# A hybrid layer with a Strassen MLP: operand sums of later passes formed in the background and kept in DRAM, fourteen up-products ahead of the first down-projection, the last rows by token blocks

## The chip, the cores and the metric

The kernel runs on one core of a Trainium2 chip. The metric is the device time of one execution in microseconds; the median of several runs is compared. The core's engines are TensorE (PE, with its weight loads PEld), VectorE (DVE), ScalarE (ACT), GpSimd (POOL) and SyncE (SP), which here only issues DMAs. Each engine executes its own list of instructions in order, and waits on semaphores for what other engines or DMAs have to finish first.

## What is computed

One decoder layer on 2064 prompt tokens (16 of them meta tokens) and 8 sample tokens, width 1024, all in float32. Two mixers, an HGRN2 gated recurrence and a convolution module, are joined by `w_out`; then comes a squared-ReLU MLP of width 4096, and a last norm.

```python
def _layer(h, ...):
    hn = _rmsnorm(h, norm1_g)
    z = jnp.einsum('btd,dc->btc', hn, w_in)
    ...
    h = h + jnp.concatenate([y_hg, y_cv], axis=-1) @ w_out
    hn2 = _rmsnorm(h, norm2_g)
    h = h + jnp.square(jax.nn.relu(hn2 @ w_up)) @ w_down
    return h, s_new, new_buf
...
y_prompt = _rmsnorm(hp[:, N_META:], final_g)
y_sample = _rmsnorm(hs, final_g)
```

## The kernel before

Every product is made from two halves of each float32 number (a high part rounded for the fast matmul, and the rest), by three matmuls: high x high, high x low, low x high. So each operand exists as a pair of tiles, written by two instructions: ACT copies and rounds the high part, DVE (or POOL) subtracts it from the source for the low part. All instructions are issued through a wrapper, so that the trace shows them all at line 146; tiles tell them apart.

The first 981 us are the **mix**: input projection, recurrence, convolution, output projection. The result h goes to DRAM, transposed (`hscr`). Then the **MLP** runs in `NPASS` = 3 passes over the tokens (688, 688 and 680 columns), each through `NG` = 16 groups of 256 hidden units.

- *Up-projection.* One group is a Strassen-Winograd product: seven products U(g, 0) to U(g, 6) of 12 matmuls, 344 (or 340) columns wide, on seven sums of the weights (formed by `up_prep` for the next group, a ring of nine slots) and seven operand sums `B11, T1, T2, B22, T3, B21, T4` of the pass's tokens. The operand sums are kept for the whole pass in `op0`, `op1` and `extra` (through `bop`), in four pairs of row tiles. `h_prep(p, i)` (lines 820 to 889) loads pair i of pass p, forms its seven sums and splits each. For passes 1 and 2 it starts with the pass before it but must wait (`until ("up", p-1)`) until that pass's last up-product is done, since the operand tiles are in use until then.
- *Down-projection.* Eight units D(g, 0) to D(g, 7) for each group, 12 matmuls each, into two pairs of PSUM banks in turn (3 and 4, 5 and 6). DVE adds each unit's result onto the accumulator `acc`, which frees the bank pair. The weights are split in pass 0 (`junk` in, `wsp` out) and stored to `down_w`; passes 1 and 2 load them from there into four slots, three units ahead.
- *Order.* PE's order is written out by hand in `seq`: U and D alternate, D one group behind; the seven products of a pass's group 0 and three of its group 1 stand ahead of D(0, 0), ten in all; in group 15 the units D(14, ..) come late, so that the up-products finish early. Everything else is background work: generators kept by class `Background` with a priority (smaller goes first) and a cost model of the engines, which places the next instruction of one of them on its engine when the model finds room. `bg.until(cond)` makes it place background work until the condition holds; what it places stands in the engines' lists ahead of whatever the program emits next. The order is thus fixed when the kernel is built.
- *End of a pass.* `residual` adds h back onto `acc`; `finish` (for each tile of 128 tokens) transposes `acc` into two banks, squares and sums on ACT, forms 1/sqrt by a chain of 11 tiny DVE steps, scales and stores. The last pass splits the columns of D(15, ..) into 0 to 424 and 424 to 680, and `finish_last` does two of its tiles together.

Of the kernel before, what the change touches and what calls it, by code (L numbers as in the profile page):

```python
# [7 lines left out]
F32 = mybir.dt.float32  # L8
# [229 lines left out]
def tile_hybrid_step(  # L238
# [32 lines left out]
    ng2 = ct([P, K8], name="ng2")  # L271
    ss0 = ct([P, 5], name="ss0")
# [22 lines left out]
    xn_t = [main.tile([P, D], F32, name=f"xn{i}") for i in range(2)]  # L295
# [33 lines left out]
    def rsqrt(src, n, scale, parts=P, bufs=None, eps=None):  # L329

        x, a, y = bufs or (sc(n)[:parts], sc(n)[:parts], keep(n)[:parts])
        if eps is None:
            V.tensor_scalar(x, src, scale, EPS, ALU.mult, ALU.add)
        else:
            V.scalar_tensor_tensor(out=x, in0=src, scalar=scale, in1=eps, op0=ALU.mult, op1=ALU.add)
# [418 lines left out]
    ring, bst, bstage, acc_of = [], [], Free([], model), []  # L754
# [4 lines left out]
    def up_prep(G_):  # L759
# [4 lines left out]
        sums.update((x, bst[i // 2].rearrange("p a n -> p (a n)")[:, (i % 2) * 512:(i % 2) * 512 + 512])  # L764
                    for i, x in enumerate(("A11", "A12", "A22")))
# [30 lines left out]
    def up_first():  # L796
        steps = up_prep(0)
        late = (20, 21, 13, 14, 15, 17)
        got = yield from take(bstage, 2)
        for n_ in [n_ for n_ in range(len(steps)) if n_ not in late] + list(late):  # L800
            if n_ == late[0]:
                bstage.give(*got)
# [17 lines left out]
    def h_prep(p, i):  # L820

        n = PN[p] // 2
        yield from until(*[("h", q, d) for q in quarters(p) for d in (i, i + 4)])
        if p == 0:
            yield from region(i // 2, 4)
        else:
            yield from until(("up", p - 1))
        if p == 0 and i < 2:
            raws = yield from take(xns, 2)
        elif p == 0:  # L830
            yield from until(("mlp",))
            raws = [acc_of[0][:, 2 * i - 4 + j] for j in range(2)]
        elif i % 2:
            yield from until(("sums", p * NG), *([("bop", p, i - 2, 1)] if i > 1 else []))
            raws = raw
        else:
            raws = yield from take(xns, 2)
        yield "sp"
        for t, k in zip(raws, (i, i + 4)):
            h_load(t, p, k)  # L840
        st_ = yield from take1(bstage)
        r = {B11: raws[0][:, 0:n], B12: raws[0][:, n:2 * n], B21: raws[1][:, 0:n], B22: raws[1][:, n:2 * n]}
        s12, s1, s2, s4 = (st_[:, a, 0:n] for a in range(4))
        g, gg = g2[:, i:i + 1], g2[:, i + 4:i + 5]
        m = PROMPT[0] - NT if p == 0 else n

        def hi_(a, src, scale=1.0):
            S.activation(bop(i, 0, a)[:, 0, 0:src.shape[1]], src, AF.Copy, scale=scale)

        def lo_(a, src):  # L850
            V.tensor_tensor(bop(i, 1, a)[:, 0, 0:n], src, bop(i, 0, a)[:, 0, 0:n].bitcast(F32), ALU.subtract)

        def lo_scaled(a, src, scale):
            w = src.shape[1]
            V.scalar_tensor_tensor(out=bop(i, 1, a)[:, 0, 0:w], in0=src, scalar=scale,
                                   in1=bop(i, 0, a)[:, 0, 0:w].bitcast(F32), op0=ALU.mult, op1=ALU.subtract)

        yield "act"
        S.activation(s12[:, 0:m], r[B12][:, 0:m], AF.Copy, scale=g)
        if p == 0:  # L860
            S.activation(s12[:, m:n], hsT[:, i], AF.Copy, scale=g)
            b22s = keep(NS)
# [1132 lines left out]
```

## Time and profile before

| | |
|---|---|
| median of 3 runs | 2521.46 us (2519.86 to 2522.32) |
| the profiled execution, its own time | 2517.77 us |
| its span in the trace | 2516.1 us |
| PE busy | 2317.9 us, 92% |
| DVE / ACT / POOL busy | 1704.1 / 1056.1 / 655.1 us |
| mean DMA rate | 155 GB/s |

The page gives each engine's busy time, the span in forty slices, and groups of instructions; the trace behind it can be asked for a stretch of time by engine (what ran, for how long, and after how long a wait for whom) and for tables of busy time by stretch. The granted clock (PEclk) is TensorE's, as a share of full speed.

### The profile page before, as it was taken

Reading aid. Unit: us, or ns where it says so; the run is one execution under the profiler, and the core shown is the slowest. Engines: PE = TensorE matmul, PEld = TensorE weight load, DVE = VectorE, ACT = ScalarE, POOL = GpSimd, SP = SyncE. Lnnn points to the kernel's source line nnn. Section 1 sums busy time; section 2 is a strip of 40 time slices with the busy share of each in tenths; the row PEclk is TensorE's granted clock in tenths of the full one; section 3 lists DMA queues with packets and bytes.
Section 4 is the critical chain, followed back from the end, with each engine's and each line's share of the span. In section 5 each row is a group of like instructions: output and inputs, shape, how many; then the busy total and the mean of one; then the engine's idle time right before and its main releaser. Section 6 shows DMA issues by size and latency. Waiting matters only on the chain.

```text
span 2516.1 us, 37234 instructions
## 1 busy us (share of the span) xinstructions
PE 2317.9 (92%) x13790; PEld 2166.6 (86%) x13790; DVE 1704.1 (68%) x3129; ACT 1056.1 (42%) x2230; POOL 655.1 (26%) x511
## 2 busy tenths in 40 slices
PE   9887889989999996899999977999999889999996
PEld 8886778967877884799999976999999879999996
DVE  6797977587669444567666676666666767666655
ACT  6444644354345233544444444333333443333332
POOL 4462514443146012244333321300100013100000
PEclk9898999999999998899999997999999989999998
DMA  8764454934564466355444453434333434333332
GB/s 296 220 198 159 143 193 140 336 144 151 204 215 152 154 235 221 101 165 165 141 141 141 142 179 101 144 107 129 105 110 108 140 120 146 118 109 110 113 106 91
DMA packets 286237, 389.35 MB, mean 155 GB/s; under 512 B 19650, under 2 KB 200455, under 8 KB 269664
## 3 DMA queue, kind: packets, MB, share of 16 engines
q1 hardware_dynamic: 285912, 386.72, 47.7%
q8 instruction: 109, 1.79, 0.3%
q14 instruction: 72, 0.59, 0.1%
q10 hardware_dynamic: 144, 0.26, 0.0%
HBM read 292.14 MB, written 95.24 MB: 154 GB/s over the span
## 4 chain that ended last, share of the span: by engine, by line
PE 52%; DVE 12%; issue 6%; DMA 4%; ACT 3%; POOL 3%; SPq 1%; DVEq 0%; POOLq 0%; ACTq 0%
PE ps L146 52%; DVE ps L146 2%; DMA junk<-in_w_down_dram 2%; DVE stat L146 2%; POOL wsp L146 1%; ACT cst L146 1%; SPq L146 1%; DVE op L146 1%; DMA bst<-in_w_up_dram 1%; DVE raw L146 1%; DVE acc L146 1%; DVE xn L146 1%; DVE cst L146 1%; POOL ups L146 1%; ACT wsp L146 1%
## 5 line engine op out<-in xcount | busy, mean ns | idle before, releaser
L146 PE MATMUL ps<-op,wsp 128*128 128x512 f32 (+6 forms) x5427 | 1068.9, 352 | 33.9 <-DVE cst L146 11.4
L146 PEld LDWEIGHTS ps<-op,wsp 128*128 128x128 f32 x5427 | 897.4, 195 | 137.7 <-DVE cst L146 11.1
L146 PE MATMUL ps<-hid,wsp 128*128 128x344 f32 (+1 forms) x4536 | 769.5, 321 | 34.1 <-DVE xn L146 13.8
L146 PEld LDWEIGHTS ps<-hid,wsp 128*128 128x128 f32 x4536 | 723.4, 189 | 44.1 <-DVE xn L146 14.5
L146 DVE TENSOR_TENSOR acc<-ps,acc 128x688 f32<-128x688 f32 (+3 forms) x368 | 313.2, 851 | 278.1 <-PE ps L146 277.5
L146 ACT ACTIVATE cst<-cst 128x344 f32<-128x344 f32 (+1 forms) x384 | 188.3, 490 | 507.3 <-DVE cst L146 501.2
L146 PE MATMUL ps<-op,ups 128*128 128x344 f32 (+1 forms) x2013 | 358.3, 326 | 34.0 <-ACT op L146 15.2
L146 PEld LDWEIGHTS ps<-op,ups 128*128 128x128 f32 x2013 | 330.9, 193 | 39.5 <-ACT op L146 16.4
L146 POOL TENSOR_TENSOR scr<-scr 128x512 f32<-128x512 f32 x172 | 230.3, 1339 | 252.1 <-ACT scr L146 232.4
L146 DVE SCALAR_TENSOR_TENSOR ps<-glu,cw,ps 128x512 f32<-128x512 f32 x292 | 219.5, 752 | 6.1
L146 POOL TENSOR_TENSOR ups<-bst,ups 128x512 fp32r<-128x512 f32 x54 | 79.8, 1488 | 442.3 <-ACT ups L146 416.7
L146 DVE TENSOR_TENSOR cst<-ps,cst 128x344 f32<-128x344 f32 (+1 forms) x336 | 171.1, 509 | 30.6 <-PE ps L146 27.1
L146 POOL TENSOR_TENSOR wsp<-junk,wsp 128x256 fp32r<-128x256 f32 x128 | 104.5, 817 | 306.4 <-ACT wsp L146 279.0
L146 POOL TENSOR_TENSOR wsp<-bst,wsp 128x512 fp32r<-128x512 f32 x42 | 62.4, 1496 | 310.7 <-ACT wsp L146 287.4
L146 DVE TENSOR_TENSOR hid<-cst,hid 128x344 fp32r<-128x344 f32 (+1 forms) x192 | 104.6, 545 | 52.6 <-ACT hid L146 51.6
L146 DVE TENSOR_TENSOR ups<-raw,ups 128x512 fp32r<-128x512 f32 x108 | 79.7, 738 | 73.1 <-ACT ups L146 72.9
L146 ACT ACTIVATE scr<-glu,cw 128x512 f32<-128x512 f32 x188 | 125.2, 715 | 1.9 <-DVE glu L146 1.9
L146 POOL TENSOR_TENSOR wsp<-raw,wsp 128x1024 fp32r<-128x1024 f32 (+1 forms) x34 | 78.7, 2314 | 79.6 <-ACT wsp L146 68.1
L146 DVE TENSOR_TENSOR wsp<-raw,wsp 128x512 fp32r<-128x512 f32 x84 | 61.7, 735 | 53.1 <-ACT wsp L146 53.0
L146 ACT ACTIVATE hid<-cst 128x344 fp32r<-128x344 f32 (+1 forms) x192 | 94.2, 491 | 6.1
L146 ACT ACTIVATE wsp<-raw 128x512 fp32r<-128x512 f32 (+1 forms) x118 | 85.9, 728 | 16.9 <-DMA raw<-in_w_in_dram 9.7
L146 ACT ACTIVATE wsp<-junk 128x256 fp32r<-128x256 f32 x128 | 52.0, 408 | 92.2 <-DMA junk<-in_w_down_dram 73.3
(231 smaller groups left out, 2133.3 us busy)
## 6 DMA issues: line engine op xcount, KB each, us to landing
wsp<-kw SPq DMA_DIRECT2D x96, 1024.0 KB, 4.8
wsp<-down_w SPq DMA_DIRECT2D x250, 256.0 KB, 2.7
bst<-in_w_up_dram SPq DMA_DIRECT2D x144, 256.0 KB, 4.2
kw<-wsp SPq DMA_DIRECT2D x32, 1024.0 KB, 5.7
down_w<-wsp SPq DMA_DIRECT2D x128, 256.0 KB, 2.4
junk<-in_w_down_dram SPq DMA_DIRECT2D x128, 128.0 KB, 2.3
raw<-in_w_in_dram SPq DMA_DIRECT2D x24, 512.0 KB, 7.2
raw<-in_w_up_dram SPq DMA_DIRECT2D x48, 256.0 KB, 3.2
```

The source lines that it names most:

```text
L146: return fn(*args, **kw)
```

## The change

- The accumulator `acc` moves to the main pool; in the mix its memory serves as the scratch buffers, of which there are then ten instead of eleven. The two `xn` tiles become wider, and the separate tile for the mask row goes.
- Pass 0: sums and most splits of its operands are emitted product by product (`h_first`, `h_rest`).
- Passes 1 and 2: `h_stage(p)`, added at U(2, 0) of the pass before with the last priority, loads the h rows, forms the 28 pairs of operand tiles (four pairs of rows by seven sums) one after another in one tile `stg`, and stores each to DRAM (`bop_d`). At each U(15, k) of passes 0 and 1 the background is first run until the staging is complete, and then `h_fetch` loads the operands of product k, whose tiles the old pass has just used for the last time, by four DMAs.
- `seq`: group 1's seven products all precede D(0, 0), so that fourteen products stand ahead of it; group 15 alternates like the others in passes 0 and 1. In the last pass group 15's products come in a row, then D(14, ..) and D(15, ..) together on columns 0 to 424, then both on 424 to 680.
- `finish` takes two neighbouring banks and works on 1024 columns at once (one square, one scaling), and the 1/sqrt is a power on POOL, in `finish_last` too. `residual` starts when all eight tiles of `acc` have been written once.

```diff
+    def split_sum(hi, lo, src, scale):
+
+        yield "act"
+        S.activation(hi, src, AF.Copy, scale=1.0 if scale is None else scale)
+        yield "dve"
+        if scale is None:
+            V.tensor_tensor(lo, src, hi.bitcast(F32), ALU.subtract)
         else:
-            raws = yield from take(xns, 2)
+            V.scalar_tensor_tensor(out=lo, in0=src, scalar=scale, in1=hi.bitcast(F32),
+                                   op0=ALU.mult, op1=ALU.subtract)
...
+        def h_stage(p):
+
+            n = PN[p] // 2
+            x, xx = yield from take(xns, 2)
+            t1, t2 = x[:, 2 * NT:2 * NT + n], xx[:, 2 * NT:2 * NT + n]
+
+            def emit(i, idx, src, scale):
+                yield from split_sum(stg[:, 0, 0:n], stg[:, 1, 0:n], src, scale)
+                yield "sp"
+                SP.dma_start(bop_d[p - 1, i, idx], flat32(stg))
+
+            for i in range(4):
+                yield "sp"
+                h_load(x, p, i)
+                h_load(xx, p, i + 4)
...
+                yield from emit(i, B11, b11, g)
+                yield from emit(i, B21, b21, gg)
+                yield from emit(i, B22, b22, gg)
+                V.tensor_tensor(t1, b12, b11, ALU.subtract)
+                S.activation(t2, b22, AF.Copy, scale=gg)
+                yield from emit(i, T1, t1, g)
...
+            xns.give(x, xx)
+            done.add(("staged", p))
+
+        def h_fetch(p, idx):
...
+            for i in range(4):
+                src = bop_d[p - 1, i, idx].rearrange("p (a n) -> p a n", a=2)[:, :, 0:n]
...
+                    o = (i % 2) * 12 + idx
+                    SP.dma_start(ops_t[i // 2].rearrange("p (s n) -> p s n", n=NT)[:, o:o + 7:6, 0:n].bitcast(F32), src)
+                done.add(("bop", p, i, idx))
...
         def finish(p, i, c0_, n):
...
-            for j in range(2):
-                S.activation(junk16[:n, 0:512], ps[0:n, bs[j], :], AF.Square, accum_out=s2[:, j:j + 1])
+            ss, r_ = sc(1)[:n], keep(1)[:n]
+            S.activation(junk16[:n], row, AF.Square, accum_out=ss)
+            yield "dve"
+            V.scalar_tensor_tensor(out=ss, in0=ss, scalar=1.0 / D, in1=emm[:n, p, i:i + 1], op0=ALU.mult, op1=ALU.add)
+            yield "pool"
+            G.tensor_tensor(r_, ss, mhalf[:n, 0:1], ALU.pow)
...
                 if g == 1:
-                    seq += us[0:3] + [x for i in range(4) for x in (ds[i], us[3 + i])] + ds[4:]
-                elif g == NG - 1:
-                    seq += [us[0], ds[0], us[1], us[2], ds[1], us[3], us[4], ds[2], us[5], us[6]] + ds[3:]
+                    seq += us + ds
+                elif g == NG - 1 and p == NPASS - 1:
+                    seq += us
...
-            seq += [D_(NG - 1, d, bl) for bl in bls for d in range(K8)]
+            seq += [D_(g, d, bl) for bl in bls for g in range(NG - 1 if p < NPASS - 1 else NG - 2, NG) for d in range(K8)]
...
                 run_unit(product(p, g, d), lambda p=p, g=g, d=d: up_epilogue(p, g, d))
+                if g == 2 and d == 0 and p < NPASS - 1:
+                    bg.add(h_stage(p + 1), 7)
+                if g == NG - 1 and p < NPASS - 1:
+                    bg.until(lambda: ("staged", p + 1) in done)
+                    h_fetch(p + 1, PRODUCTS[d][3])
```

How this moves instructions is seen at three places. The first is DVE at the end of pass 0: the acc additions `acc<-ps,acc` there belong to D(13, 6), D(13, 7) and D(14, 0), `hid`, `cst` and `ups` to the up-projection. Before:

```order
L146 TENSOR_TENSOR acc<-ps,acc 128x688
L146 TENSOR_TENSOR hid_7714<-cst,hid_7714 128x344
L146 TENSOR_TENSOR acc<-ps,acc 128x688 x2
L146 TENSOR_TENSOR cst<-ps,cst 128x344 x2
L146 TENSOR_TENSOR raw_85<-bst_7386,raw_84 128x512
L146 TENSOR_TENSOR raw_84<-raw_84,bst_7387 128x512
L146 TENSOR_TENSOR acc<-ps,acc 128x688
```

And after, from D(13, 6)'s addition on; the rows up to the next addition of `acc` go on in the same manner, with six more splits into `stg`:

```order
L146 TENSOR_TENSOR acc<-ps,acc 128x688
L146 TENSOR_TENSOR hid_7724<-cst,hid_7724 128x344
L146 TENSOR_TENSOR acc<-ps,acc 128x688
L146 SCALAR_TENSOR_TENSOR stg<-xn_90,vec,stg 128x344
L146 SCALAR_TENSOR_TENSOR xn_91<-xn_90,ng_78,xn_91 128x344
L146 TENSOR_TENSOR stg<-xn_91,stg 128x344
L146 SCALAR_TENSOR_TENSOR xn_90<-xn_91,vec 128x344
L146 TENSOR_TENSOR stg<-xn_90,stg 128x344
L146 SCALAR_TENSOR_TENSOR xn_91<-xn_90,ng_78,xn_91 128x344
L146 TENSOR_TENSOR stg<-xn_91,stg 128x344
L146 SCALAR_TENSOR_TENSOR stg<-xn_90,vec,stg 128x344
```

Between D(13, 7)'s addition and D(14, 0)'s, which were neighbours, now stand eleven splits into `stg` with the sums that they need.

The second place is SP's list of DMAs in the same part of the program. Before, storing the split down weights (`down_w<-wsp`), loading the next (`junk<-in_w_down_dram`) and loading h rows for the operand sums alternate:

```order
L146 DMA junk<-in_w_down_dram 128x2x128
L146 DMA down_w<-wsp_86 128x512
L146 DMA junk<-in_w_down_dram 128x2x128
L146 DMA raw_84<-hscr 128x688
L146 DMA raw_85<-hscr 128x688
L146 DMA down_w<-wsp_86 128x512
L146 DMA junk<-in_w_down_dram 128x2x128
L146 DMA down_w<-wsp_86 128x512
L146 DMA junk<-in_w_down_dram 128x2x128
```

After, from the last store of the staging on:

```order
L146 DMA bop_d<-stg 128x688 x7
L146 DMA op_83<-bop_d 128x2x344 x2
L146 DMA op_84<-bop_d 128x2x344 x2
L146 DMA raw_85<-in_w_up_dram 128x4x128
L146 DMA bst_7385<-in_w_up_dram 128x4x128 x2
L146 DMA bst_7386<-in_w_up_dram 128x4x128
L146 DMA down_w<-wsp_87 128x512
L146 DMA junk<-in_w_down_dram 128x2x128
L146 DMA op_83<-bop_d 128x2x344 x2
L146 DMA op_84<-bop_d 128x2x344 x2
L146 DMA down_w<-wsp_87 128x512
L146 DMA junk<-in_w_down_dram 128x2x128
```

The loads of the h rows and the sums are gone from here; each product's four fetches (`op<-bop_d`) stand ahead of the next pair of weight DMAs, and so on for all seven products.

The third place is PE at the start of pass 1: `ident,acc` are the transposes of `finish`, `hid,wsp` the first down-units, `op,wsp` and `op,ups` the up-products. Before, the end of the tenth product, the last transposes and D(0, 0), with the next product behind it:

```order
L146 MATMUL ps<-op_82,wsp_87 128x344 x6
L146 MATMUL ps<-op_83,wsp_87 128x344 x6
L146 MATMUL ps<-op_82,wsp_88 128x344 x6
L146 MATMUL ps<-op_83,wsp_88 128x344 x6
L146 MATMUL ps<-ident,acc 128x128 x8
L146 MATMUL ps<-ident,acc 48x128 x8
L146 MATMUL ps<-hid_7713,wsp_86 128x344 x6
L146 MATMUL ps<-hid_7714,wsp_86 128x344 x6
L146 MATMUL ps<-op_82,wsp_88 128x344 x6
L146 MATMUL ps<-op_83,wsp_88 128x344 x6
```

After, the end of the fourteenth product, the last transposes and the first down-units:

```order
L146 MATMUL ps<-op_83,wsp_88 128x344
L146 MATMUL ps<-op_84,wsp_88 128x344
L146 MATMUL ps<-op_83,wsp_88 128x344
L146 MATMUL ps<-extra,wsp_88 128x344 x9
L146 MATMUL ps<-ident,acc 48x128 x8
L146 MATMUL ps<-hid_7723,wsp_87 128x344 x6
L146 MATMUL ps<-hid_7724,wsp_87 128x344 x6
L146 MATMUL ps<-hid_7723,wsp_87 128x344 x6
L146 MATMUL ps<-hid_7724,wsp_87 128x344 x6
```

Four more products stand ahead of the first down-unit, and the down-units of group 0 follow each other.

## Rows read from the trace of the kernel before

**Rows 1.** The page, part 1: busy time, share, instructions; then part 2's row.

```profile
PE 2317.9 (92%) x13790; PEld 2166.6 (86%) x13790; DVE 1704.1 (68%) x3129; ACT 1056.1 (42%) x2230; POOL 655.1 (26%) x511
...
PE   9887889989999996899999977999999889999996
```

**Rows 2.** Table of stretches, PE to POOL busy with instruction counts, clock, DMA.

```profile
core 0: us, PE busy (x) PEld busy (x) DVE busy (x) ACT busy (x) POOL busy (x), PEclk, DMA share, GB/s
0.00:981.00 981.00, 902.24 (x5004) 774.25 (x5004) 698.85 (x1375) 438.00 (x927) 368.16 (x263) 0.95 0.59 199
981.00:1041.00 60.00, 29.59 (x123) 24.93 (x124) 40.28 (x82) 30.06 (x72) 7.21 (x8) 0.66 0.34 95
...
1445.40:1494.00 48.60, 45.17 (x273) 42.52 (x272) 35.58 (x55) 21.10 (x48) 15.56 (x18) 1.00 0.57 179
1494.00:1554.00 60.00, 31.82 (x170) 27.93 (x168) 45.68 (x141) 27.18 (x64) 2.93 (x2) 0.76 0.37 123
1554.00:1955.00 401.00, 397.45 (x2493) 396.63 (x2494) 253.31 (x392) 147.94 (x287) 52.09 (x36) 0.99 0.39 116
...
1998.00:2050.60 52.60, 31.22 (x169) 28.26 (x167) 42.98 (x138) 24.83 (x60) 3.01 (x2) 0.75 0.36 111
...
2491.00:2516.10 25.10, 6.03 (x29) 3.87 (x28) 15.77 (x73) 7.36 (x22) 0.00 (x0) 0.58 0.29 111
```

**Rows 3.** Time line of PE around the first change of pass.

```profile
1458.59 2.05 PE L146 MATMUL ps<-hid,wsp 128*128 128x344 f32 x12
1460.47 2.07 PE L146 MATMUL ps<-op,wsp 128*128 128x344 f32 x12
...
1464.27 7.72 PE L146 MATMUL ps<-hid,wsp 128*128 128x344 f32 x48
...
1494.01 1.11 PE L146 MATMUL ps<-op,wsp 128*128 128x344 f32 x6
...
1511.19 0.94 PE L146 MATMUL ps<-op,wsp 128*128 128x344 f32 x2 [4.78 <-DVE op L146]
...
1554.04 3.81 PE L146 MATMUL ps<-hid,wsp 128*128 128x344 f32 x12 [6.79 <-DVE xn L146]
```

**Rows 4.** The page, part 5: groups of instructions, mean ns after the comma.

```profile
L146 DVE TENSOR_TENSOR acc<-ps,acc 128x688 f32<-128x688 f32 (+3 forms) x368 | 313.2, 851 | 278.1 <-PE ps L146 277.5
...
L146 DVE TENSOR_TENSOR hid<-cst,hid 128x344 fp32r<-128x344 f32 (+1 forms) x192 | 104.6, 545 | 52.6 <-ACT hid L146 51.6
...
L146 ACT ACTIVATE hid<-cst 128x344 fp32r<-128x344 f32 (+1 forms) x192 | 94.2, 491 | 6.1
```

**Rows 5.** The page, part 6: DMA issues, KB each and us to landing.

```profile
kw<-wsp SPq DMA_DIRECT2D x32, 1024.0 KB, 5.7
down_w<-wsp SPq DMA_DIRECT2D x128, 256.0 KB, 2.4
```

**Rows 6.** DMA issues from 1470 to 1560 us, columns as in rows 5.

```profile
raw<-hscr SPq DMA_DIRECT2D x4, 344.0 KB, 5.2
```

**Rows 7.** Table of a busy stretch in the mix, columns as in rows 2.

```profile
440.00:480.00 40.00, 39.12 (x328) 38.54 (x328) 28.97 (x59) 17.93 (x38) 19.31 (x11) 1.00 0.99 318
```

**Rows 8.** Time line of the end, PE and DVE.

```profile
2484.13 1.25 PE L146 MATMUL ps<-ident,acc 128*128 128x128 f32 x10
...
2499.86 1.97 PE L146 MATMUL ps<-ident,acc 128*128 128x128 f32 x8 [5.31 <-DVE xn L146]
...
2502.83 0.16 DVE L146 SCALAR_TENSOR_TENSOR stat<-stat,emm 128x1 f32<-128x1 f32 x1
...
2505.20 1.41 DVE L146 SCALAR_TENSOR_TENSOR xn<-ps,kept,fg 128x512 f32<-128x512 f32 x2
...
2511.18 1.40 DVE L146 SCALAR_TENSOR_TENSOR xn<-ps,kept,fg 40x512 f32<-40x512 f32 x2
```

**Rows 9.** Time line of the hand-over to the MLP: SP's queue and PE.

```profile
1002.23 12.06 SPq L146 DMA_DIRECT2D emm<-mscr  x19
...
1026.44 3.81 PE L146 MATMUL ps<-op,wsp 128*128 128x344 f32 x12 [6.52 <-DVE cst L146]
```

More of the change, by code (lines that the diff above doesn't have):

```diff
@@ L914, in tile_hybrid_step, with h_rest @@
+    def h_rest():
+        yield from until(("sum0", 2), ("sum0", 3))
+        yield from region(1, 4)
+        for idx in SUMS[:-1]:
+            yield from first_split((2, 3), idx)
+        yield from until(("mlp",))
+        yield from first_split(range(4), T4)
+        xns.give(*xn_t[:2])
+        bstage.give(*bst)
+        done.add(("rest",))
     with tc.manual_schedule():
@@ L916, in tile_hybrid_step @@
         G.memset(ones, 1.0)
+        G.memset(mhalf, -0.5)
         with ExitStack() as p1:
@@ L1587, in tile_hybrid_step @@
         hid = [[mlp_p.tile([P, 2, 2 * NT], F32R, name=f"hid{a}{b}") for b in range(2)] for a in range(2)]
-        msb = mlp_p.tile([P, 2 * NT], F32, name="msb")
-        acc = mlp_p.tile([P, K8, 2 * NT], F32, name="acc")
-        acc_of.append(acc)
+        stg = mlp_p.tile([P, 2, NT], F32R, name="stg")
+        up_raws[1] = [b[:, 0:512] for b in scr.take(3)]
         done[("mlp",)] = model.t["pe"]
@@ L1628, in residual @@
         def residual(p):
-            yield from until(*[("st", q) for q in quarters(p)])
+            yield from until(*[("st", q) for q in quarters(p)], *[("acc", p, k) for k in range(K8)])
+            t, msb = yield from take(xns, 2)
             yield "sp"
@@ L1637, in residual @@
             for k in range(K8):
-                yield from until(("acc", p, k))
-                t = yield from take1(xns)
                 yield "sp"
@@ L1677, in finish @@
             xns.give(t)
         def finish_last(p, i, c0_):
-            bs = yield from bank(4)
+            pair = []
+            while not pair:
+                pair = [b for b in (0, 2) if b in banks.items and b + 1 in banks.items] if 4 in banks.items and \
+                    7 in banks.items else []
+                if not pair:
+                    yield "poll"
+            bs = [4, pair[0], 7, pair[0] + 1]
+            for b in bs:
+                banks.items.remove(b)
             ts = raw
@@ L1725, in finish_last @@
             bg.add(last_gains(), 9)
-            r_ = yield from rsqrt(ss, 2, 1.0 / D, eps=emm[:, p, i:i + 2])
+            r_ = keep(2)
+            V.scalar_tensor_tensor(out=ss, in0=ss, scalar=1.0 / D, in1=emm[:, p, i:i + 2], op0=ALU.mult, op1=ALU.add)
+            yield "pool"
+            G.tensor_tensor(r_, ss, mhalf, ALU.pow)
+            yield "dve"
             yield from until(("gains", 2))
```

258 lines of the change are left out of this document (124 added, 134 removed).

## The prediction

> **What bounds the kernel now.** I read the page first: TensorE (PE) is busy 2317.9 us of 2516.1, and its row in forty slices is full except for a few places [rows 1]. The table of stretches sizes those places [rows 2]. Steady MLP work has next to no slack: 397.45 busy us in the 401.00 from 1554 to 1955. At the two changes of pass PE is busy 31.82 of 60.00 us and 31.22 of 52.60, at a mean granted clock of 0.76 and 0.75 of full speed. The last 25.10 us hold 6.03 us of PE, and where the mix hands over (981 to 1041) it has 29.59 of 60.00. So a gain has to come from one of those holes, and anything that stops PE in steady work is paid in full. The time line of PE gives the unit: 12 matmuls 344 wide, an up-product or a down-unit, start 1.88 us apart (1458.59 to 1460.47), while the same 12 take 3.81 us when they follow a wait [rows 3].
>
> **Where the background work went.** Before, the operand sums of the next pass are formed at the pass change, and PE waits on DVE and ACT for them (the 4.78 us ahead of 1511.19). After, they are formed during the running pass through one tile, `stg`, and stored. The order on DVE decides how much of that is hidden: of the 28 splits of pass 1's operands, 17 stand among pass 0's work and 11 stand together between the acc addition of D(13,7) and that of D(14,0), since the planner is made to finish them after U(15,0). In pass 1 it is 23 and 5. DVE runs its list in order, so D(14,0)'s bank stays full until all 11 are through. PE can still issue U(15,0), D(14,0), U(15,1), D(14,1), U(15,2): 5 x 1.88 = 9.4 us. Then D(14,2) needs that bank.
>
> **What one split costs.** ACT writes the high part, DVE the low, the tile is stored, and the next split may write only when the store has landed. The same operations on 344 columns take 0.491 us (ACT) and 0.545 us (DVE) [rows 4]. A store of two 128 x 344 tiles is 344 KB; a store of 256 KB lands in 2.4 us and one of 1024 KB in 5.7 [rows 5], so between them 2.4 + 88/768 x 3.3 = 2.8. With 0.15 us for the hand-overs a cycle is 0.49 + 0.55 + 2.8 + 0.15 = 4.0 us. Eleven cycles are 44; the last store need not have landed (-2.8); the next pair's two rows must come in between, 5.2 us at a pass change [rows 6], part of it under the last splits of the old pair, so +3; the first acc addition of 0.851 us [rows 4] closes it: about 45 us after D(13,7). PE has work for 9.4, so it stops for **36.5 us** (31 with cycles of 3.5, 48 with 5). In pass 1, five cycles, no new pair: 20 - 2.8 + 0.85 + 2.2 for the rest of the store that the first of them waits for = 20.2, less 9.4: **10.8 us** (8 to 16).
>
> **What the fetches cost.** After each U(15,k) come four DMAs, 4 x 344 KB = 1.41 MB, on SP, and SP's order puts them ahead of the next down-projection weight. Pass 0 then still stores one weight piece and loads one (256 KB and 128 KB, 0.39 MB) for every unit, and the group's up-weights, 1.05 MB, go through the same queue. From the end of the staging to the last fetch that is 7 x 1.80 + 1.05 = 13.7 MB. A busy stretch of the mix moves 318 GB/s at a DMA share of 0.99 [rows 7], so 320 is what I take: 43 us. The weight for D(15,2) comes after the seventh fetch, and the units that PE can do before it, from D(14,2) on, are twelve: 23 us. PE waits the difference, **20 us**; in pass 1 there is no w_down load or split, 7 x 1.66 + 1.05 = 12.6 MB, 40 us against 23: **17 us**. Both between 10 (if the four weight slots stand fuller than SP's order says) and 24 (280 GB/s). The Trainium skill (DMA: Bandwidth & Descriptors, section Bandwidth) has 425 GB/s for one 16 MB transfer into SBUF; by that figure, an estimate, the queue would last 32 us and the waits be 9 and 7, but the row shows 318 with the engines full.
>
> **What the pass change gives back.** From 1494.01 to the first down-unit of pass 1 at 1554.04 PE passes 60.0 us [rows 3] and does ten products (10 x 1.88 = 18.8) and 48 transposes (4.8 us at 0.1 each, from ten in 1.25 with the last one's drain [rows 8]): 36.4 us are lost. After, 14 products need no sums, and only the finishing of pass 0's rows (transposes, ACT square, DVE scale) stands beside them, with 26.4 us of products to hide it. I leave 7.5 us of waits: six finishing tiles, of which four can be under the products, and one unit at half clock. Gain **29 us**; bounds 22 and 34. The 52.6 us of the second change [rows 2] hold the same work, 29.0 lost: gain **21 us** (15 to 27). The thirteen down-units before the first change take 29.7 us (1464.27 to 1494.01) where 13 x 1.88 is 24.5 [rows 3], since DVE forms sums among their additions: **5 us** more.
>
> **What the end gives back.** From 2491.00 to 2516.10 the last tiles finish one after another: transposes at 2499.86, scale at 2505.20, the last tile's scale at 2511.18, some 6 us for each tile [rows 8], 2.4 of it (2502.8 to 2505.2) a chain of tiny DVE steps that a power on POOL replaces. After, tiles 0 to 3 belong to columns 0 to 424, whose D(15) units are done while 16 units on 256 columns still run, so they finish under PE work; only tiles 4 and 5 stay behind the last unit. That leaves a last addition, transposes, squares, the power, the scale and a store: 8.5 us by the durations of the same steps. Against it, PE has 2.6 us of transposes inside its work and 1.5 us for the narrower units. 25.1 - 8.5 - 2.6 - 1.5 = **12.5 us** (9 to 14). POOL's power on one or two columns stands in no row; the smallest and dearest bounds are a DVE step of 0.16 us and some 2 us, the chain it replaces: I take 0.7, inside the 8.5.
>
> **The rest.** The 40 splits that lie in steady work add 0.5 us each on ACT and DVE, which have room (253.31 and 147.94 us busy in 401.00) [rows 2]; each can still hold ACT or DVE for the landing of the previous store when two stand close, and PE can run two units ahead: **+4 us** (0 to 12). Two more restarts of PE after a wait, 3.81 - 1.88 = 1.9 us each [rows 3]: **+4**. The mix has ten scratch buffers where it had eleven, and three conv taps move from ACT to DVE: 0, but 8 us either way, since PE's 902.24 us there leave 79 us of waits that a new order may move [rows 2]. The hand-over to the MLP still waits for 19 small loads of `emm` that occupy SP 12.06 us and hold the up-weights back (PE's 6.52 us ahead of 1026.44) [rows 9]; the first sums are ready earlier but that queue is not: 0 (-6 to +3). The two pairs that come before the first down-unit are counted in the pass change.
>
> **Sum**, against the profiled execution's own 2517.77 us: +36.5 + 10.8 + 20 + 17 = 84.3 of new waits; -29 - 21 - 5 - 12.5 = -67.5; +4 + 4. Net +24.8: 2542.6. That execution lies 3.7 us under the median of the runs, 2521.46, so on the runs' scale **2546 us**, 1.0% slower. A difference under 0.2%, 5 us, is one that a measurement of this kernel can't tell from none.
>
> **Rivals.** *The fetches hold nothing back.* If weights come through between them (four slots ahead, DMA at a share of only 0.57 there [rows 2]), the 37 us go and 2509 us, faster, is left. Against it: SP's order, and seven times 1.41 MB in a stretch that has 0.39 MB a unit now. The Trainium skill (same page, section Queues, rings and completion order) says that descriptors of one ring are consumed in ring order, which no row here shows and which would speak against this rival. *The lump is short too*: if a store lets go of the tile in well under 1 us, or the staging is through by U(15,0), all 84 us go: 2462, or 2480 if half of the price of the fetches stays, the change doing what it says. Against it: 2.4 us for smaller stores [rows 5]. *The pass change still waits.* The row sums of pass 0 can't be finished before its last addition, and D(0,0) may not write `acc` before the last transposes; if residual additions and squares pile up on DVE and ACT at that place as now, 40 of the 50 us stay lost: 2586 us, slower. It decides from the point where finishing six tiles takes DVE and ACT more than the 26.4 us of products.
>
> **How the numbers follow.** My sum 0.63 (with its bounds 2522 to 2572), fetches free 0.18, all short 0.07, pass change as before 0.12. Range: the low end takes in the free fetches with some luck in the mix, 2503; the high end the third rival, 2586. Faster: the rivals with free fetches and a sliver of the sum, 0.23; within 5 us of now 0.08; slower 0.69.
>
> **What would show it.** After U(15,2) of pass 0 PE stands still some 36 us, with the releaser DVE acc, while ACT and DVE show eleven `stg` pairs 4 us apart; after it, waits on weights (ACT or POOL wsp in pass 0, DMA wsp in pass 1) of 20 and 17 us, with DMA shares over 0.9. Fourteen products then run with under 10 us of gaps. The last addition of acc lies 8 to 9 us before the end. I am wrong if `stg` pairs lie under 2 us apart, if the DMA share in the fetch stretch stays near 0.6 with no PE wait, or if the pass change keeps 30 us of gaps.

## The result, and the profile after

The changed kernel takes **2561.68 us** (median of 4 runs, 2560.96 to 2564.89) against 2521.63 us for the kernel before (4 runs, 2519.86 to 2522.32): a ratio of 1.0162, 95% interval 1.0145 to 1.018. It is 1.6% slower; the forecast was 2546 us, 1.0% slower. Its profiled execution took 2564.89 us, 47.1 us more than that of before; the medians are 40.0 us apart, so 7 us of the difference between the two traces is scatter from one execution to the next.

To see where, both traces are cut at the same work. Every group's last up-product U(g, 6) ends in nine matmuls on the tile `extra`, and what is done between two such places is the same in both kernels if they are chosen well: U(2, 6) to U(14, 6) is the inside of a pass, U(14, 6) to U(2, 6) of the next pass a pass change with both its sides. The times between them, read from the starts of those matmuls, with the sum that the prediction's terms make for the same stretch:

```
                           before    after   change   forecast
start to U(2,6), pass 0    1087.2   1089.5    +2.3      0
inside of pass 0            352.3    363.6   +11.3     +4, all three passes
change from pass 0 to 1     163.3    187.3   +24.0     36.5 + 20 + 2 - 29 - 5 = +24.5
inside of pass 1            345.6    349.9    +4.3
change from pass 1 to 2     150.4    162.8   +12.4     10.8 + 17 + 2 - 21     =  +8.8
inside of pass 2            341.4    342.7    +1.3
U(14,6) of pass 2 to end     75.9     67.5    -8.4     -12.5
span                       2516.1   2563.2   +47.1     +24.8
```

The page of the changed kernel, part 1, and part 6's row of the new stores, answers to [rows 1] and [rows 5]:

```profile
PE 2326.5 (91%) x13790; PEld 2170.7 (85%) x13790; DVE 1684.5 (66%) x2906; ACT 1055.4 (41%) x2199; POOL 666.1 (26%) x529
...
bop_d<-stg SPq DMA_DIRECT2D x56, 344.0 KB, 2.7
```

PE's busy time is nearly the same (8.6 us more); some 38 us of waiting have come in, though DVE has less to do. The store lands in a median of 2.7 us, where 2.8 had been worked out from [rows 5]. Where PE waits is seen on its time line at the end of pass 0 (after [rows 3]):

```profile
1467.74 2.07 PE L146 MATMUL ps<-op,ups 128*128 128x344 f32 x12
1501.11 3.78 PE L146 MATMUL ps<-hid,wsp 128*128 128x344 f32 x12 [31.30 <-DVE acc L146]
...
1513.51 3.81 PE L146 MATMUL ps<-op,ups 128*128 128x344 f32 x12 [4.42 <-DVE cst L146]
...
1528.90 2.34 PE L146 MATMUL ps<-hid,wsp 128*128 128x344 f32 x12 [1.17 <-ACT wsp L146]
1535.83 5.82 PE L146 MATMUL ps<-hid,wsp 128*128 128x344 f32 x24 [4.59 <-DVE acc L146]
1542.86 12.45 PE L146 MATMUL ps<-hid,wsp 128*128 128x344 f32 x72 [1.21 <-ACT wsp L146]
1555.14 3.46 PE L146 MATMUL ps<-op,wsp 128*128 128x344 f32 x21
```

The line at 1467.74 is U(15, 2), the fifth unit that could be issued; D(14, 2) starts 31.30 us after it had ended, released by the addition of D(14, 0). In that time ACT does this (its time line):

```profile
1478.28 0.58 ACT L146 ACTIVATE stg<-xn,vec 128x344 fp32r<-128x344 f32 x1 [5.18 <-DMA xn<-hscr]
1481.81 0.58 ACT L146 ACTIVATE stg<-xn,vec 128x344 fp32r<-128x344 f32 x1 [2.96 <-DMA bop_d<-stg]
1485.33 0.58 ACT L146 ACTIVATE stg<-xn,vec 128x344 fp32r<-128x344 f32 x1 [2.94 <-DMA bop_d<-stg]
```

One split each 3.5 us, most of it the wait for the store before it. In pass 1, where five are left, the same place reads:

```profile
2016.25 3.81 PE L146 MATMUL ps<-hid,wsp 128*128 128x344 f32 x12 [10.62 <-DVE acc L146]
2019.86 2.60 PE L146 MATMUL ps<-op,wsp 128*128 128x344 f32 x12
2027.34 3.78 PE L146 MATMUL ps<-hid,wsp 128*128 128x344 f32 x12 [4.88 <-DVE raw L146]
```

The table of stretches (columns as in [rows 2]) shows what follows: the stretch of the fetches, the new pass's fourteen products, and the fetches of pass 1.

```profile
1501.00:1555.10 54.10, 42.60 (x216) 40.42 (x217) 23.58 (x34) 14.55 (x31) 13.63 (x16) 0.83 0.93 310
1555.10:1598.90 43.80, 34.80 (x218) 32.72 (x217) 25.75 (x44) 21.89 (x43) 6.09 (x7) 0.95 0.33 109
...
2016.20:2069.30 53.10, 42.12 (x217) 40.95 (x218) 24.03 (x34) 9.77 (x19) 2.97 (x2) 0.83 0.87 292
```

The first is 18 units, 33.8 us of matmuls at 1.88 us each, in 54.0 us (D(14, 2) at 1501.11 to the next pass's first product at 1555.14), with the DMA engines 93% busy at 310 GB/s. Of the 20.2 us more, PE is idle for 11.4, in the four waits shown above behind the one of 31.30; the rest is units that run at a granted clock of 0.50 behind a wait, as the one at 1501.11, 3.6 us long. In pass 1 the same 18 units take 53.0 us, and three of the waits are for down weights:

```profile
2044.83 3.65 PE L146 MATMUL ps<-hid,wsp 128*128 128x344 f32 x12 [2.22 <-DMA wsp<-down_w]
...
2050.22 2.12 PE L146 MATMUL ps<-hid,wsp 128*128 128x344 f32 x12 [1.74 <-DMA wsp<-down_w]
2054.42 15.02 PE L146 MATMUL ps<-hid,wsp 128*128 128x344 f32 x84 [2.08 <-DMA wsp<-down_w]
2069.28 3.89 PE L146 MATMUL ps<-op,ups 128*128 128x340 f32 x24
```

The second row of the table answers to the 60.0 us of [rows 2], with four more products in it: 43.8.

### The profile page after: what moved, and what is told of

It reads as the page before. It is cut to its first block, busy times and chain, and to the rows that moved or that the text cites. A ratio compares the mean times of both kernels' runs of the same rounds, so it can differ in the third digit from the quotient of the medians.

```text
span 2563.2 us, 37257 instructions
## 1 busy us (share of the span) xinstructions
PE 2326.5 (91%) x13790; PEld 2170.7 (85%) x13790; DVE 1684.5 (66%) x2906; ACT 1055.4 (41%) x2199; POOL 666.1 (26%) x529
## 4 chain that ended last, share of the span: by engine, by line
PE 46%; DVE 20%; issue 11%; DMA 10%; ACT 5%; POOL 4%; SPq 2%; POOLq 0%; ACTq 0%; DVEq 0%
PE ps L146 46%; DVE ps L146 7%; DMA junk<-in_w_down_dram 4%; SPq L146 2%; DVE stat L146 2%; POOL wsp L146 2%; DMA bst<-in_w_up_dram 2%; DVE acc L146 2%; ACT cst L146 1%; DMA bop_d<-stg 1%; DVE cst L146 1%; POOL ups L146 1%; DVE I L146 1%; DVE kept L146 1%; DVE raw L146 1%
## 5 line engine op out<-in xcount | busy, mean ns | idle before, releaser
L146 PE MATMUL ps<-hid,wsp 128*128 128x344 f32 (+2 forms) x4512 | 779.9, 324 | 95.3 <-DVE acc L146 61.9
L146 DVE TENSOR_TENSOR acc<-ps,acc 128x688 f32<-128x688 f32 (+4 forms) x424 | 346.5, 818 | 319.4 <-PE ps L146 259.6
L146 POOL TENSOR_TENSOR acc<-acc 128x512 f32<-128x512 f32 x169 | 225.1, 1332 | 244.4 <-ACT acc L146 227.6
L146 DVE TENSOR_TENSOR cst<-ps,cst 128x344 f32<-128x344 f32 (+1 forms) x336 | 170.9, 509 | 19.2 <-PE ps L146 15.7
L146 ACT ACTIVATE acc<-glu,cw 128x512 f32<-128x512 f32 x185 | 123.5, 715 | 1.6 <-DVE glu L146 1.6
L146 ACT ACTIVATE wsp<-raw 128x512 fp32r<-128x512 f32 (+1 forms) x118 | 85.9, 728 | 10.8 <-DMA raw<-in_w_in_dram 6.6
```

Of the source, the lines that this page charges most:

```text
L146: return fn(*args, **kw)
```

## The experiments

Two theories stood behind the forecast: the splits left over at U(15, 0) run at the pace of the store's landing and hold PE (the lump); and the fetches hold the weights of the following down-units. Twelve kernels were run. All are edits of the changed kernel, but for two that start from the kernel before. The stretches of the table above are used throughout; the spans are those of one profiled execution each, and a time given without an interval is that of a single execution. Such stretches scatter by some 3 us: the inside of pass 2, which no edit concerns, took 340.3 to 343.5 us in all fourteen kernels.

**No operands formed at all.** The staging and the fetches leave; the rest of the change stays.

```diff
-                    bg.add(h_stage(p + 1), 7)
...
-                    bg.until(lambda: ("staged", p + 1) in done)
-                    h_fetch(p + 1, PRODUCTS[d][3])
+                    for i in range(4):
+                        done.add(("bop", p + 1, i, PRODUCTS[d][3]))
```

> The changed kernel without the staging and the fetches: passes 1 and 2 take pass 0's operand sums as they stand in the tiles, so the forming, storing and fetching of their own is left out. Theory (the two lumps of staging and the fetches ahead of the weights hold PE): the waits of 33 + 11 us and 20 + 19 us at the ends of passes 0 and 1 go, and some 8 us inside the passes: 2562 - 91 = 2471 us, PE without a wait over 2 us from U(15,0) to the end of either pass. Rival (the down weights or the up weights hold PE there anyway, as group 15 now runs alternating): waits of 10 us or more stay in those stretches and the time is over 2500.

2461.59 us, with the kernel before at 2523.99: the theory's side, 9 us below its figure, and the longest wait of PE left there is 2.1 us. The pass changes took 135.6 and 129.7 us (187.3 and 162.8 in the changed kernel), the insides of passes 0 and 1 356.7 and 343.2 (363.6 and 349.9). So without any work on the operands of passes 1 and 2, which the kernel before still does, the change would be 62 us faster than it, and staging and fetching cost 100 us of run time; of the 103 us by which the spans differ, 85 lie at the two pass changes, 14 inside passes 0 and 1.

**Two staging tiles.** The splits alternate between `stg` and the unused end of `bst1`; the order stays.

```diff
+                stg = stgs[sn[0] % 2]
+                sn[0] += 1
                 yield from split_sum(stg[:, 0, 0:n], stg[:, 1, 0:n], src, scale)
```

> The changed kernel with two staging tiles in turn; the order on all engines stays, eleven and five splits still stand together. Theory (each split waits for the landing of the store before it, 3.5 us a cycle): a cycle falls to 1.75 us, PE's wait for D(14,0)'s addition from 31 to 12 to 15 us in pass 0 and from 10.6 to about 4 in pass 1, the fetch waits stay at 20 and 19: 2562 - 23 = 2539 us. Rival (the splits' own instructions and their hand-overs take the 3.5 us): cycles stay over 3 us and the time at 2555 to 2562.

2541.41 us. PE's time line at the same two places of this kernel:

```profile
1485.55 3.45 PE L146 MATMUL ps<-hid,wsp 128*128 128x344 f32 x12 [16.62 <-DVE acc L146]
...
1993.85 3.60 PE L146 MATMUL ps<-hid,wsp 128*128 128x344 f32 x12 [3.37 <-DVE acc L146]
```

16.6 and 3.4 us where it was 31.3 and 10.6. All engines' lists are the same in both kernels, and the lump lost 15 and 7 us with the second tile: the landing of the stores set its pace. What is left is the splits' own chain and one wait of 5.5 us for the next pair's rows.

**Even staging.** One tile; over the 49 up-products of groups 8 to 14 the number of splits that must have been placed rises evenly to 28.

```diff
+                if 8 <= g < NG - 1 and p < NPASS - 1:
+                    quota = -(-28 * ((g - 8) * 7 + d + 1) // (7 * (NG - 1 - 8)))
+                    bg.until(lambda: nst[p + 1] >= quota)
```

> The changed kernel with one staging tile, but the planner is made to place one or two splits beside each up-product of groups 8 to 14, so that none is left at U(15,0). Theory (the cost is that eleven and five stand in front of one acc addition): the waits of 31 and 10.6 us go, the even splits cost 0 to 6 us a pass inside, the fetch waits stay at 20 and 19: 2562 - 36 = 2526 us. Rival (each split stops ACT and DVE for the landing of the store before it wherever it stands, and PE with them): the same 40 us return as many waits of 0.5 to 2 us in groups 8 to 14, 2555 us or more.

2559.17 us: the theory missed, and the rival's time came (its reason, the landing, did not bear out, as the kernels with all three mends show below). The pass changes fell from 187.3 and 162.8 to 153.5 and 148.8, but the insides rose from 363.6 and 349.9 to 393.1 and 362.7. The 31 us that were seen in one piece came back in small ones. What PE waited for from 1240 to 1462 us, groups 8 to 14 of pass 0, in the kernel with even staging (engine, line, for whom; us, times, longest); in the changed kernel the waits in these groups come to 7.2 us:

```profile
PE ps L146 <- ACT wsp L146: 12.7, 5, 3.7
PE ps L146 <- DVE acc L146: 6.8, 4, 4.0
PE ps L146 <- DVE cst L146: 2.8, 1, 2.8
```

**Late fetches.** One fetch DMA goes behind each following unit.

```diff
         def h_fetch(p, idx):
+            fpend.extend((p, idx, i) for i in range(4))
...
+            h_fetch_next()
             for f in old:
                 f()
```

> The changed kernel with the fetches issued one DMA behind each following unit instead of four at once behind each up-product; the lumps stay. Theory (seven times four fetches stand ahead of the weights on SP): the waits on weights of 20 and 19 us fall under 5 us each, the lumps of 31 and 10.6 stay: 2562 - 32 = 2530 us. Rival (the DMA engines are full in that stretch, whatever the order): the waits stay, or move to the first products of the next pass, 2550 us or more.

2542.10 us, between the two. The change from pass 1 to 2 fell from 162.8 to 145.5 us; the one from pass 0 to 1 only from 187.3 to 183.7. Not all of the 17.3 us is the fetches': the planner left four splits instead of five behind D(13, 7)'s addition, and PE's wait for D(14, 0)'s was 4.26 us instead of 10.62. The 18 units from D(14, 2) to the next pass took 48.2 and 43.6 us (54.0 and 53.0 in the changed kernel).

**No fetches, staging kept.**

```diff
-                    h_fetch(p + 1, PRODUCTS[d][3])
+                    for i in range(4):
+                        done.add(("bop", p + 1, i, PRODUCTS[d][3]))
```

> The changed kernel with the staging and its stores but without the fetches: passes 1 and 2 take pass 0's operand sums from the tiles. Theory (the fetches hold the weights and so PE at the ends of passes 0 and 1): the two lumps stay (PE's waits of 31 and 10.6 us), behind them the waits on weights go, and from U(14,6) to U(2,6) of the next pass 187 us become 170 and 163 become 142: 2562 - 38 = 2524 us. Rival (what the late-fetch run gained, 20 us, is all that the fetches cost): 2540 us.

2539.45 us, the rival's time. The change from pass 1 to 2 took 142.0 us, 20.8 less than in the changed kernel; the one from pass 0 to 1 only 3.2 less. Neither is the price of the fetches, since the planner placed other work differently too. In pass 1 four splits are left instead of five, and the lump is shorter. In pass 0 the waits between U(14, 6) and U(0, 6) fell by 14.4 us (71.2 + 53.9 against 66.4 + 44.3), but the next stretch, to U(2, 6), rose by 11.3, where this kernel's last transposes stand later in PE's order and wait for the scaling of the tile before. PE in pass 0 and pass 1:

```profile
1503.13 3.78 PE L146 MATMUL ps<-hid,wsp 128*128 128x344 f32 x12 [31.52 <-DVE acc L146]
...
1548.91 3.94 PE L146 MATMUL ps<-op,wsp 128*128 128x344 f32 x24
...
1586.38 1.09 PE L146 MATMUL ps<-ident,acc 128*128 128x128 f32 x8 [3.06 <-DVE xn L146]
1590.14 3.68 PE L146 MATMUL ps<-ident,acc 128*128 128x128 f32 x16 [2.66 <-DVE xn L146]
1596.51 1.06 PE L146 MATMUL ps<-ident,acc 128*48 128x128 f32 x8 [2.69 <-DVE xn L146]
...
2006.79 3.81 PE L146 MATMUL ps<-hid,wsp 128*128 128x344 f32 x12 [6.73 <-DVE acc L146]
...
2048.22 5.78 PE L146 MATMUL ps<-op,ups 128*128 128x340 f32 x36
```

The price is read from the 18 units between, D(14, 2) to the next pass's first product, which stand in the same order in all these kernels. With the kernel without operands and the one with room, two tiles and fetches at once (below) all four cases of lump and fetches are there:

```
18 units, start to start, us                pass 0                     pass 1
lump and fetches (changed kernel)           1501.11-1555.14  54.0      2016.25-2069.28  53.0
lump, no fetches (this kernel)              1503.13-1548.91  45.8      2006.79-2048.22  41.4
fetches, no lump (room, two tiles)          1485.26-1532.53  47.3      1988.78-2031.25  42.5
neither (no operands formed)                1456.84-1494.81  38.0      1933.98-1968.74  34.8
```

So the fetches cost 8.2 and 11.6 us behind a lump, 9.3 and 7.7 without one: 17 to 20 us in both passes together. And the lump leaves another 7 to 11 us behind its own wait, with fetches or without. Each case is one execution, so 3 us here or there mean little.

**All three mends, and the same with one tile.** Even staging and late fetches, with two tiles and with one.

> The changed kernel with all three: two staging tiles, splits placed evenly in groups 8 to 14, fetches one DMA behind each unit. Theory (what even staging cost with one tile, 28 us in pass 0 and 15 in pass 1, was ACT standing at the next split for the landing of the store before it, with the down weights' splits behind it): with two tiles that store is an older one and has landed, groups 8 to 14 lose at most 6 us a pass more than without staging, the lumps are gone and the fetch waits as in the late-fetch run: 2490 to 2510 us, faster than before. Rival (the splits' own work on ACT and DVE is too much there): the 43 us stay, about 2537 us.

> The same with one staging tile. Theory of the landing: the 28 + 15 us of the even-staging run stay, 2559 - 22 = 2537 us, 30 us or more above the run with two tiles. Rival (work, not landing): the same time as with two tiles within 8 us.

2530.32 us (ratio to before 1.0039, 1.0026 to 1.0051) with two tiles, 2529.0 us with one: spans 2527.1 and 2527.3. The theory missed: the engines' lists are the same in both, and with splits spread evenly the second tile is worth nothing; the inside of pass 0 stays at 391.1 and 392.5 us. The pass changes are short, 149.7 and 133.0 us with two tiles. In the one with two tiles, ACT's waits in the same stretch hold none for the landing of a store; the first after those for DVE's `cst` are

```profile
ACT wsp L146 <- DMA junk<-in_w_down_dram: 21.6, 11, 3.9
ACT bst L146 <- DMA xn<-hscr: 11.0, 2, 10.3
ACT stg L146 <- issue: 8.1, 2, 5.2
```

A forced split is written into ACT's and DVE's lists at once, in front of other work, and waits there for its own sources, once 10.3 us for the rows of the next pair. How such a wait reaches PE is seen in three lines of this kernel, DVE, ACT and PE in turn:

```profile
1406.85 1.03 DVE L146 TENSOR_TENSOR bst<-xn,bst 128x344 fp32r<-128x344 f32 x1 [2.02 <-ACT bst L146]
```

```profile
1409.37 1.01 ACT L146 ACTIVATE cst<-cst 128x344 f32<-128x344 f32 x2 [2.55 <-DVE cst L146]
```

```profile
1411.26 3.81 PE L146 MATMUL ps<-hid,wsp 128*128 128x344 f32 x12 [3.41 <-ACT wsp L146]
```

DVE stands 2.02 us for the split's high part from ACT, with additions to `cst` behind it; ACT stands 2.55 us for one of these, with a weight split (`wsp`) behind it; and PE waits 3.41 us for that and then runs its next unit at a granted clock of 0.50, 3.81 us long. That chains like this one make up the whole of the 34 us by which the inside of pass 0 exceeds the run without operands was not shown.

**Placed where the planner finds room, one tile.** The planner is told not to count the landing; nothing is forced, and all 28 splits are placed by group 11.

```diff
+                t_ = model.cur.t
                 SP.dma_start(bop_d[p - 1, i, idx], flat32(stg))
+                model.cur.t = t_
```

> The changed kernel with one line: the planner no longer counts the landing of a store before the next split, so that all 28 splits are placed where it finds room, by group 11, and none is left at U(15,0) in either pass; one tile, fetches as in the changed kernel. Theory (forcing puts a split in front of waiting ACT and DVE work, room does not): groups 2 to 14 lose at most 10 us a pass more than without staging, the ends of the passes lose the lumps, 43 to 8 and 21 to 4 us: 2562 - 52 + 10 = 2520 us. Rival (a split costs PE 0.5 to 1 us wherever it stands, as in the even-staging runs): 28 + 15 us are lost inside and the time is 2550 us or more.

2577.59 us, the slowest of all: the pass changes are at 146.2 and 138.1, the insides at 418.7 and 374.5.

**The same with two tiles, fetches at once and late.**

> The run with room, two tiles and late fetches, but with four fetches at once behind each up-product as in the changed kernel; no lump stands before them. Theory (order on SP): the waits on weights come back in full, 15 to 20 us in each pass, 2509 + 35 = 2544 us. Rival (the number of bytes, not their order, sets that wait): 2509 to 2515 us.

> The same with two staging tiles and the fetches one DMA behind each unit. Theory: inside the passes under 10 us in both together over the run without operands, and the ends of the passes as in the run of the three mends (150 and 133 us from U(14,6) to U(2,6), against 136 and 130 without operands): 2462 + 10 + 18 = 2490 us, the fastest so far. Rival (a split costs 0.5 to 1 us wherever it stands): 2520 us.

2524.32 us with fetches at once, 2509.27 us with late ones (ratio to before 0.9939, 0.9921 to 0.9957). The first differs from the kernel with one tile in the second tile alone, with the same lists on all engines, and is 53 us faster: inside pass 0 381.8 us against 418.7. What ACT waited for from 1200 to 1470 us, first with one tile, then with two:

```profile
ACT stg L146 <- DMA bop_d<-stg: 82.4, 19, 9.0
```

```profile
ACT bst L146 <- DMA bop_d<-bst: 12.3, 3, 5.2
ACT stg L146 <- DMA bop_d<-stg: 9.1, 3, 3.9
```

So the landing counts wherever splits follow each other closely in the lists, in a lump or in the open, and not where they are spread: in the run with even staging, one tile and late fetches the last 21 stores of pass 0 go out from 1302 to 1481 us, one in nine microseconds. Late fetches against fetches at once: 142.5 and 132.4 us at the pass changes against 146.2 and 137.9, and 15 us in the run time, less than half of what the theory of order asked for and more than the rival's 6; only 9 of the 15 lie at the pass changes, the rest where the fetches have no part. Without operands these stretches took 135.6 and 129.7. So fetches at once, with no lump before them, cost 11 and 8 us at the pass changes, and late ones 7 and 3.

**Fourteen products alone, in the kernel before.**

```diff
                 if g == 1:
-                    seq += us[0:3] + [x for i in range(4) for x in (ds[i], us[3 + i])] + ds[4:]
+                    seq += us + ds
```

> The kernel before with nothing changed but seven instead of three products of group 1 ahead of D(0,0), fourteen in all. Theory (at a pass change PE waits first for the operand sums, 34 and 24 us, then for the last rows of the old pass, 15 and 13 us; the order helps the second alone): 16 to 24 us of the two second waits go, the first stay: 2524 - 20 = 2504 us. Rival (the four more products only wait for their own sums, and both waits are one): 2518 us or more.

2525.58 us against 2520.75 of the kernel before: no gain. The pass changes took 165.9 and 151.5 us (163.3 and 150.4 before). The products are issued ahead of D(0, 0), but the old finish is not done by then; PE at that place in this kernel:

```profile
1563.51 1.05 PE L146 MATMUL ps<-ident,acc 128*48 128x128 f32 x4 [4.66 <-DVE xn L146]
1571.52 17.64 PE L146 MATMUL ps<-hid,wsp 128*128 128x344 f32 x96 [6.96 <-DVE xn L146]
```

**Fourteen products, the new finish and the new end, in the kernel before.** The change's `finish`, `finish_last` and order of the last pass are put in as well; the operand sums stay as they were.

> The kernel before with fourteen products ahead of D(0,0), the changed finish (neighbouring banks, one square, the power on POOL) and the changed order of the last pass, without any staging or fetch. Theory (these parts bring gains by themselves, and the staging is what costs): 2504 - 8.5 for the end (29.0 us lost behind the last product before, 20.5 after) = 2495 us, and a few us less at the pass changes by the shorter finish. Rival (the gains need the operands to be ready): 2512 us or more.

2502.34 us, ratio to before 0.9926 (0.9911 to 0.9941), between the theory's 2495 and the rival's 2512. The pass changes take 156.9 and 145.9 us and the end 67.7 instead of 75.9. D(0, 0) no longer waits for a scaling; the one wait over 1 us left among the group's eight down-units is

```profile
1564.17 11.60 PE L146 MATMUL ps<-hid,wsp 128*128 128x344 f32 x72 [1.09 <-ACT acc L146]
```

This version and the one with room, two tiles and late fetches beat both kernels. They were not measured side by side, and their intervals overlap, so which of them is faster stays open.

## Why the prediction was right, and where its sizes were off

**The lump: right.** The forecast was 36.5 us in pass 0 and 10.8 in pass 1; PE waited 31.30 and 10.62 behind the named bank, with the named releaser. (The terms given for pass 0 add up to 35.7, not 36.5.) The cycle was 3.5 us where 4.0 had been taken: 0.58 on ACT and a wait of 2.94, of which DVE's 0.58 is part, so 2.4 us are left for store and hand-overs where 2.95 had been taken. The run with two tiles shows the cause. What the forecast did not have is that the lump also leaves 7 to 11 us behind it, in units at the lower clock and in waits; it had one restart of 2 us in each pass.

**The fetches: half the price, and the sum met by luck.** 20 and 17 us had been forecast, and the two stretches did lose 20.2 and 19.2 us (54.0 and 53.0 for 33.8 of work). But without the fetches the same units still take 45.8 and 41.4 us. The fetches' own share is 8.2 and 11.6, in pass 0 below the stated bound of 10; the rest is what the lump leaves behind, 7.8 and 6.7, and 4.1 and 0.9 that are lost with neither. The step that failed is the way the wait was to arise: PE was to run twelve units, 23 us, and then stand for a down weight. It stood for down weights only 2.4 us in pass 0 (ACT `wsp`) and 6.0 in pass 1 (DMA `wsp`), and in pass 0 it stopped at the fourth unit already, at 1513.51, for an addition to `cst`. That stood on DVE behind the next group's up weights, whose loads SP had issued behind the first four fetches:

```profile
1510.73 0.69 DVE L146 TENSOR_TENSOR raw<-bst,raw 128x512 f32<-128x512 f32 x1 [8.98 <-DMA bst<-in_w_up_dram]
```

In pass 1 the 4.88 us ahead of 2027.34 came about in the same way, behind 7.96 us of DVE. The prediction had counted these loads as bytes alone. Without the fetches the longest such wait of DVE in pass 0 is 3.0 us. That the order on SP makes most of the price is seen without a lump: fetches at once take 47.3 and 42.5 us, late ones 41.9 and 36.7, none 38.0 and 34.8. The rival of fetches that hold nothing back did not come, but was nearer than it looked: the fetches' 20 us are about half of the 37. The bandwidth taken, 320 GB/s, stood at 310 and 292 in the two stretches; the figure of 425 GB/s that the Trainium skill has (DMA: Bandwidth & Descriptors, section Bandwidth) for one large transfer was not reached by this mix of 344 KB reads and 256 KB stores.

**The pass change: somewhat too much.** A gain of 29 and 21 us was forecast with 7.5 us of waits left; between the last down-unit and D(0, 0) 43.8 us passed, 12.6 more than the 31.2 of products and transposes (26.4 + 4.8), and 42.7 in the second change, 11.5 more. So the gain there was 23.8 and 17.5. The term for waits left was 3.5 to 5 us too small: the transposes of a tile wait for the scaling of the one before, and four of the six tiles in the first change, three in the second, came with waits of 0.5 to 2.6 us each. In the first change all terms together gave +24.0 against +24.5. That is luck: the lump was 5 us and the fetches 12 us smaller than forecast, the other loss of the 18 units (12 us, where one restart of 2 had been taken) 10 us and the waits here 5 us larger.

**The inside of the passes: this is the term that failed.** +4 us had been taken for the splits in steady work, with 12 as the bound, on the ground that ACT and DVE have room on average. It was +11.3, +4.3 and +1.3. The run without operands has 356.7 and 343.2 us inside passes 0 and 1, so 7 us in each of them are the splits'. The 4 us more in pass 0 that are there without any split may be scatter for the greater part: the two kernels made from the one before, with the same work and the same order of PE inside the pass, took 355.4 us there, not 352.3. The busy share says nothing on how an instruction fits into a list that is worked off in order. Every run that placed all 28 splits inside paid more: 22 to 36 us in pass 0 against the run without operands, 0.8 to 1.3 us for each split (62 us with one tile and tight packing), where the seventeen of the changed kernel cost 0.4. Which chain of waits makes up this price was followed in one place only, above; the cause as a whole stays open.

**The end: 8.4 us instead of 12.5.** What stands behind the last addition was sized well: it starts at 2554.52 and the span ends at 2563.2, 8.7 us against 8.5, with the power on POOL at 0.70 us as taken.

```profile
2554.52 0.42 DVE L146 TENSOR_TENSOR acc<-ps,acc 128x256 f32<-128x256 f32 x1
...
2557.15 0.70 POOL L146 TENSOR_TENSOR kept<-kept,mhalf 128x2 f32<-128x2 f32 x1 [6.50 <-DVE kept L146]
```

What was left out are PE's waits inside its last work: two of 1.51 us where the transposes of a tile wait for the scaling that frees their banks, and three of 0.3 to 0.54 us for additions:

```profile
2538.66 1.09 PE L146 MATMUL ps<-ident,acc 128*128 128x128 f32 x8 [1.51 <-DVE xn L146]
...
2542.64 1.05 PE L146 MATMUL ps<-ident,acc 128*40 128x128 f32 x8 [1.51 <-DVE xn L146]
```

**Mix and hand-over: 0 forecast, +2.3 measured.** Other kernels with the same mix needed 1083.8 to 1090.7 us for this stretch, so 2.3 is within what it scatters.

In sum, the misses of the stretches went one way, though terms inside the first change missed both ways: 13 us inside the passes, 4 at the second change, 4 at the end, 2 at the start make the 22 by which the spans' difference of 47.1 exceeds the 24.8 of the sum. Some 7 of these 22 lie in the two executions that were profiled, one the slowest of its four, the other faster than all four of its kind: by the medians the change is 40.0 us, 15 more than the sum, and the time 16 us above the 2546 forecast. Of the rivals, the short lump and the pass change that still waits did not come; the fetches were not free, but cost half.

## What to carry to other kernels

Work that a planner moves into the background is paid for at the place where it must be complete: look in the order for what is left there, and for who stands behind it. A tile that is written, stored and written again runs at the pace of the store's landing as soon as two uses are close; a second tile was worth 20 us in the lump and 53 us where the splits were packed in the open, and nothing where the stores were spread to some nine us apart. Where two causes meet in one stretch, take away each alone and both together before giving either its price: here a sum that met to 0.2 us (20 forecast, 20.2 lost) hid one term at half its size and another that was not foreseen. When a change bundles several edits, price each alone: here the order, the finish and the end brought 0.7%, and staging and fetching took that and more.

## What was not expected of the hardware

The price of a split in the open: with ACT busy 42% and DVE 67% of the span, the 28 splits of a pass cost PE 22 us in pass 0 and 12 us in pass 1 in the best of these runs, against the run without operands: 0.8 and 0.4 us each. A split is one ACT and one DVE instruction of some 0.5 us and a store; 16 sums on DVE and 8 scaled copies on ACT come to the 28. In pass 0 ACT, POOL and SP also split and store the down weights, in pass 1 they don't; that this makes the difference was not tested.

What a long wait of PE leaves behind: after the 31 us of the lump in pass 0 the next 18 units took 45.8 us without any fetch, 7.8 more than where no lump stood before them.
